# Sample's state updates moved up, the norms' roots split, sample's gates tied: one step of a hybrid decoder layer

## The chip, the cores and the metric

The kernel runs on one core of a Trainium2 chip. The metric is device time in microseconds: the median of several runs of the same program, and beside it one profiled execution, whose trace is the source of every row shown. Two programs are compared on the same chip.

## The reference

One inference step of a layer with two mixers. A prompt of 2048 tokens and a sample of 8 sequences of 8 new tokens go through the same weights.

```python
z = rmsnorm(x, norm_w) @ w_in
q, k, v, qb, kb, vb, g_lr, gate_a, gate_b = split(z)
o_a = attend(q, k, v)                      # three dilated windows, mixed by their softmax sums
log_a = log_sigmoid(g_lr @ w_gate_up + b_gate) / 16
o_b, s_fin = gla_chunked(qb / 8, kb, vb, log_a, s0)     # gated linear attention, 4 heads
o_b = rmsnorm(o_b, gla_norm_w)             # per head of 128
mixed = concat([o_a * silu(gate_a), o_b * silu(gate_b)])
y = x + mixed @ w_out
```

In the linear attention a state of 64 x 128 per head is decayed and added to: `state = exp(b_last) * state + k_decayed^T v`. For the prompt it starts at zero and runs over 16 chunks of 128 tokens; for the sample each of the 8 sequences brings its own state, reads it for its outputs, updates it once, and the new state is an output of the program. Each head's output then goes through a root mean square norm, so for every token and head a sum of squares and its inverse root are needed before the last projection.

## The kernel before

The program is one stream of operations written by Python generators. `weave` (L370) takes from several generators the one that is furthest behind its share, and so lays the parts into each other: a `host` (a projection on TensorE) with others beside it; a generator that yields WAIT is passed over. From this order a planner, which keeps its own clock of every engine, fixes the order of the instructions on each engine by when they can start. Each engine then runs its own instructions strictly in order; so does SP, which issues all DMAs.

Tiles live in pools. A pool takes a stretch of on-chip memory; a pool that is opened later can take the stretch of one that was closed. Tiles of one tag share a fixed number of buffers (`bufs`), and a new tile of a tag waits until the readers of the one that had its buffer are done.

The phases from 942 us on, which the change touches:

- **The gb projection** (942 to 1076 us). Host is `rest("gb")` (L1542): 16 prompt tiles through `project`, whose 24 matmuls per tile (L1161) add up `acc_gb`; ACT copies the result out (`zgb`, L757) and SP stores it. Beside it run the end of the prompt's linear attention (`gla_prompt`, with `chunk` for 128 tokens: state and output matmuls, the state's addition on DVE at L1331, and `gla_out`, which stores the output and takes the sums of squares of the four heads into columns of `ob_ss`, L346), the loading of the two halves of w_out (`load_w("o0")`, `load_w("o1")`, L664 and L665), and the sample's linear attention, `sample_gla` (L1400).
- **`sample_gla`** opens the pool sg1 and runs in this order: load the state S0, form decays and scores, then for each pair of heads p the outputs O_s (PSUM), their copy `ob_s` (L1467), store and sums of squares. Only when both pairs are done come the state updates (L1477 to L1503): for each pair p and half q of the sequences, and each head j, POOL builds a block `vx` of 64 x 4 x 128, in which each row holds its token's values in the place of its own sequence and zeros elsewhere (L1484); two matmuls (L1490) form U_s; POOL decays the old state (L1495) and DVE adds U_s (L1501). `vx` has one buffer. Two yields stand in each of the four rounds. After each pair SP stores the new state (L1506), and at the end sg1 is closed.
- **The seam** (L1553 to L1770). The five pools of the linear attention are closed, and cb (two buffers each) and cb1 (one) are opened in that stretch. cb1 holds, among others, `va`, `ob_rs`, `ident16`, the exponentials `sa`, and sample's own gates and outputs. `rsqrt` (L117) takes the 68 columns of `ob_ss` (4 for sample, 64 for 16 tiles) in one go to `ob_rs`: six small instructions, DVE, two on ACT (logarithm and exponential), three on DVE. `first_mixes` forms the mixes of tiles 0 and 1.
- **The output phase** (1102 us to the end). `prompt_out` (L1747) runs over the 16 tiles. `combine(t)` (L1680) loads the three attention branches (oc), gates (zl, `gates` L1579: a clamp on DVE, three passes on ACT into `sa`, two reductions on DVE, then `p2` and `smx`) and head outputs (obl, scaled by the roots on ACT, L1606), forms `mix`, and `parts_of` (L1612) splits it into two halves of 16 bits, mt: one ACT copy, one DVE subtraction. `turned` transposes mt on PE (tm, L1625) and ACT copies it out (mh, L1626); `finish` runs 48 matmuls Y (L1667) per tile, adds the residual on DVE (xr, L1674) and stores (L1678). Tile t+2 is combined while tile t is multiplied. At t = 8 in program order sample's gates and scaled outputs are formed (L1750); they are used before the last tile. Beside it runs sample's attention over its cache: keys (k, tk, L1842 and L1845), scores R, and values, 28 loads sv (L1922) into three buffers, each read by matmuls OS (L1896).

The planner brought sample's clamp and scaling forward, ahead of tile 0's matmuls: `zl_s` and `obl_s` in the trace.

Of the kernel before, what the change touches and what calls it, by code (L numbers as in the profile page):

```python
# [18 lines left out]
P = 128  # L19
# [33 lines left out]
def tile_hymba(ctx: ExitStack, tc: tile.TileContext, A: dict):  # L53
# [340 lines left out]
    with ExitStack() as c1:  # L394
# [867 lines left out]
        )  # L1262
        gpools = (gl, gt, ps_O, ps_S, ps_P, gq)

        masks = gc.tile([P, len(LEVELS), 32], F32, name="gmask")
        scan_m = gc.tile([P, 256], F32, name="scan_m")
        wgu = gc.tile([17, 256], F32, name="wgu")
# [28 lines left out]
        POOL.memset(ob_ss[:], 1.0)  # L1296

        def at_heads(t):
            c = 0 if t == "s" else 4 * (t + 1)
            return ob_ss[:, c : c + 4]  # L1300

        def chunk(core, gc):
            c, r0 = gc % 2, gc * P
            ebv = core.eb[:].rearrange("p a (c s) -> p a c s", s=P)
            vb = vbs.pop(gc)
            old, new = Sbd[gc % 2], Sbd[(gc + 1) % 2]
            U = ps_O.tile([P, 512], F32, name=f"U_{gc}", tag="O")
            for h in range(4):
                p, j = divmod(h, 2)
                PE.matmul(  # L1310
                    U[64 * j : 64 * j + 64, p * P : (p + 1) * P],
                    core.kdt[:, c, 64 * h : 64 * h + 64], vb[:, h * P : (h + 1) * P],
                    start=True, stop=True,
                )
            O = ps_O.tile([P, 512], F32, name=f"O_{gc}", tag="O")
            for p in range(2):
                if gc:
                    PE.matmul(
                        O[:, p * 256 : (p + 1) * 256], core.qe[:, p, c * P : (c + 1) * P],
                        old[:, p, :], start=True, stop=False,  # L1320
                    )
                for j in range(2):
                    h = 2 * p + j
                    PE.matmul(
                        O[:, h * P : (h + 1) * P], full[:, 4 * j + 2 * c + p, :],
                        vb[:, h * P : (h + 1) * P], start=(gc == 0), stop=(gc == 0 or j == 1),
                    )
            for p in range(2):
                for j in range(2):
                    sl = slice(64 * j, 64 * j + 64)  # L1330
                    DVE.scalar_tensor_tensor(  # L1331
                        new[sl, p, j * P : (j + 1) * P], old[sl, p, j * P : (j + 1) * P],
                        ebv[sl, p, c, P - 1 : P],
                        U[sl, p * P : (p + 1) * P], ALU.mult, ALU.add,
                    )
            gla_out(gq, O, P, r0, f"c{gc}", at_heads(gc))
            mixed.add(gc)

        vbs = {}

# [59 lines left out]
        def sample_gla():  # L1400
# [9 lines left out]
            yield from upto("vb", "s")  # L1410
            vb = g1.tile([NS, 512], F32, name="vb_s")
            SP.dma_start(vb[:], vb_d[S : S + NS, :])
            own = g1.tile([P, 512], F32, name="own", tag="vx")
            DVE.memset(own[:], 0.0)
            E, ks, qs = (
                own[:, 0:128].rearrange("p (i c) -> p i c", i=2), own[:, 128:256], own[:, 256:320]
# [26 lines left out]
            qe, eb, kdt, Am = core.qe, core.eb, core.kdt, core.Ac  # L1443
            so = A["state_gla_sample"][0]
            ebv = eb[:].rearrange("p a (b t) -> p a b t", t=8)
            for p in range(2):
                O = ps_O.tile([P, 512], F32, name=f"O_s{p}", tag="O")
                for j in range(2):
                    h, js = 2 * p + j, slice(64 * j, 64 * j + 64)
# [19 lines left out]
                for j in range(2):  # L1469
                    h = 2 * p + j  # L1470
                    jk = gq.tile([P, P], BF16, name=f"obq_s{h}", tag="obq", bufs=2)
                    ACT.activation(
                        jk[:NS], ob[:, j * P : (j + 1) * P], AF.Square,
                        accum_out=at_heads("s")[:NS, h : h + 1],
                    )
                yield
            for p in range(2):  # L1477
                for q in range(2):
                    sq = S0[p][:, 4 * q : 4 * q + 4, :]
                    U = ps_O.tile([P, 512], F32, name=f"U_s{p}{q}", tag="O")  # L1480
                    for j in range(2):
                        h = 2 * p + j
                        vx = g1.tile([NS, 4, P], F32, name=f"vx_{h}_{q}", tag="vx")
                        POOL.tensor_tensor(  # L1484
                            vx[:],
                            vb[:, h * P : (h + 1) * P].unsqueeze(1).to_broadcast([NS, 4, P]),
                            bm[:, 4 * q : 4 * q + 4].unsqueeze(2).to_broadcast([NS, 4, P]),
                            ALU.mult,
                        )
                        PE.matmul(  # L1490
                            U[64 * j : 64 * j + 64], kdt[:NS, 0, 64 * h : 64 * h + 64], vx[:],
                            start=True, stop=True,
                        )
                        if j == 0:
                            POOL.tensor_tensor(  # L1495
                                sq, sq,
                                ebv[:, p, 4 * q : 4 * q + 4, 7:8].to_broadcast([P, 4, P]),
                                ALU.mult,
                            )
                            yield  # L1500
                    DVE.tensor_tensor(  # L1501
                        sq, sq, U[:].rearrange("p (b v) -> p b v", b=4), ALU.add
                    )  # L1503
                    yield
                for j in range(2):
                    SP.dma_start(  # L1506
                        so[:, 2 * p + j].rearrange("b k v -> k b v"),
                        S0[p][64 * j : 64 * j + 64],
                    )
# [53 lines left out]
        va = cb1.tile([P, 2], F32, name="va")  # L1563
        for i, c_ in enumerate((2048.0 / M_SCALE, 1.0 / (P_SCALE * W_SCALE * H_SCALE * V_SCALE))):
            DVE.tensor_scalar(va[:, i : i + 1], powers["v"][:], c_, None, ALU.mult)
        ob_rs = cb1.tile([P, 4 * (NT + 1)], F32, name="ob_rs")
        rsqrt(cb1, ob_rs[:], ob_ss[:], 1.0 / 128.0, P, 4 * (NT + 1), "ob")

        def scales(c):

# [27 lines left out]
        def normed(t, n, rows):  # L1598

            pool, tag = (cb1, "obs") if t == "s" else (cb, "ob")  # L1600
            ob = pool.tile([P, 512], F32, name=f"obl_{t}", tag=tag)
            SP.dma_start(ob[:n], ob_d[rows, :])
            c = 0 if t == "s" else 4 * (t + 1)
            for h in range(4):
                s = slice(h * P, (h + 1) * P)
                ACT.activation(ob[:n, s], ob[:n, s], AF.Copy, scale=ob_rs[:n, c + h : c + h + 1])  # L1606
            return ob

        ident16 = cb1.tile([P, P], F16, name="ident16")
        DVE.tensor_copy(ident16[:], ident[:])  # L1610

        def parts_of(tag, mix):  # L1612

            mt = cb.tile([P, 2, D], F16, name=f"mt_{tag}", tag="mt")
            ACT.activation(mt[:, 0], mix[:], AF.Copy)
            DVE.tensor_tensor(mt[:, 1], mix[:], mt[:, 0], ALU.subtract)
            return mt

        def turned(tag, mt):
# [127 lines left out]
        def prompt_out():  # L1747
            for t in range(NT):
                rows = slice(t * P, (t + 1) * P)
                if t == NT // 2:  # L1750
                    at_s = slice(S, S + NS)
                    mixes["s"] = gates("s", NS, at_s), normed("s", NS, at_s)
                if t == NT - 1:
                    while "attended" not in mixed:
                        yield WAIT
# [289 lines left out]
```

## Time and profile before

| | |
|---|---|
| median of 3 runs | 1342.91 us (1339.44 to 1348.45) |
| the profiled execution, its own time | 1343.97 us |
| its span, first to last instruction | 1342.2 us |
| PE busy | 1210.9 us, 90% |
| DVE, ACT, POOL busy | 887.4, 848.5, 617.3 us |
| DMA | 285.39 MB, mean 213 GB/s |
| mean granted clock of TensorE | 0.977 |

Busy times are sums over the whole span; what a change is worth is read from the stage that it touches. In the rows below, `out<-in` are the program's names with numbers left out, L is a line of the kernel, `x16` a count; the bracket at the end is the idle time of that engine just before and what ended it. PEld is the loading of the stationary operand, SPq the queue of DMA issues. The shares of the DMA engines can come out a little over 1.

### The profile page before, as it was taken

Reading aid. Unit: us, or ns where it says so; the run is one execution under the profiler, and the core shown is the slowest. Engines: PE = TensorE matmul, PEld = TensorE weight load, DVE = VectorE, ACT = ScalarE, POOL = GpSimd, SP = SyncE. Lnnn points to the kernel's source line nnn. Section 1 sums busy time; section 2 is a strip of 40 time slices with the busy share of each in tenths; the row PEclk is TensorE's granted clock in tenths of the full one; section 3 lists DMA queues with packets and bytes.
Section 4 is the critical chain, followed back from the end, with each engine's and each line's share of the span. In section 5 each row is a group of like instructions: output and inputs, shape, how many; then the busy total and the mean of one; then the engine's idle time right before and its main releaser. Section 6 shows DMA issues by size and latency. Waiting matters only on the chain.

```text
span 1342.2 us, 27996 instructions
## 1 busy us (share of the span) xinstructions
PE 1210.9 (90%) x9754; PEld 727.2 (54%) x9754; DVE 887.4 (66%) x2317; ACT 848.5 (63%) x2281; POOL 617.3 (46%) x596
## 2 busy tenths in 40 slices
PE   3798999999899798998999988899999949999998
PEld 1343565566556545666677665567555424544443
DVE  6357767788868937678672885666542368889741
ACT  5655787878669858787895454455762366556520
POOL 0066554687758733654222865665423123233210
PEclk9999999999999999999999999999999969999999
DMA  8959866668955798989785564553552688898752
GB/s 259 253 155 243 227 190 150 179 208 225 223 173 177 210 271 285 264 265 227 199 200 174 185 217 124 165 147 108 149 200 84 233 273 294 303 384 319 298 187 79
DMA packets 251807, 285.39 MB, mean 213 GB/s; under 512 B 125441, under 2 KB 160338, under 8 KB 251666
## 3 DMA queue, kind: packets, MB, share of 16 engines
q1 hardware_dynamic: 251666, 283.60, 70.6%
q8 instruction: 77, 1.26, 0.4%
q14 instruction: 64, 0.52, 0.1%
HBM read 183.12 MB, written 75.24 MB: 192 GB/s over the span
## 4 chain that ended last, share of the span: by engine, by line
PE 44%; DVE 13%; DMA 10%; POOL 8%; issue 7%; ACT 5%; SPq 1%; POOLq 0%; DVEq 0%; ACTq 0%
PE acc_gb L1161 6%; PE Y L1667 6%; PE acc_qkb L1161 4%; PE acc_vb L1161 3%; PE acc_g L1161 3%; DMA T<-qp_d 3%; PE O L492 3%; PE s L459 2%; PE t L477 2%; PE acc_k L1161 2%; POOL k L1027 2%; PE acc_q L1161 2%; PE acc_v L1161 2%; PE sc_e L289 2%; DVE p L467 1%
## 5 line engine op out<-in xcount | busy, mean ns | idle before, releaser
L1161 PEld LDWEIGHTS <-hr 128*128 128x128 f16 x1824 | 174.5, 99 | 128.8 <-issue 13.2
L1161 PEld LDWEIGHTS <-hl 128*128 128x128 f16 x1248 | 121.5, 99 | 148.5 <-issue 24.4
L444 POOL TENSOR_TENSOR pt<-p,pt 128x512 f16<-128x512 f32 (+1 forms) x80 | 94.0, 1175 | 224.3 <-ACT pt L443 187.0
L470 ACT ACTIVATE p<-p,o 128x256 f32<-128x256 f32 (+1 forms) x320 | 148.5, 468 | 52.2 <-DVE o L467 50.7
L1667 PE MATMUL Y<-w_o,mh 128*128 128x512 f16 x768 | 176.4, 379 | 2.7 <-DVE xr L1674 1.6
L1027 POOL TENSOR_TENSOR k<-k,qb 128x512 f32<-128x512 f32 x96 | 132.2, 1391 | 27.9 <-DMA qb<-q_d 12.3
L1667 PEld LDWEIGHTS <-mh 128*128 128x128 f16 x768 | 71.6, 98 | 89.6 <-issue 9.9
L477 PE MATMUL t<-ident,p 128*128 128x128 f32 x600 | 107.6, 281 | 6.6 <-ACT p L470 2.9
L492 PEld LDWEIGHTS <-pt 128*128 128x128 f16 x1200 | 82.7, 99 | 47.1 <-issue 9.5
L492 PE MATMUL O<-v,pt 128*128 128x128 f16 x944 | 88.6, 223 | 20.6 <-POOL pt L444 6.1
L467 DVE CUSTOM_DVE_ANT_0 p<-s,m3w,scl_s 128x128 f32<-128x128 f32 (+1 forms) x256 | 89.2, 395 | 26.0 <-PE s L459 7.4
L1161 PE MATMUL acc_g<-w_g,hr 128*128 128x272 f16 (+1 forms) x768 | 103.4, 282 | 3.1 <-ACT vbs L761 3.1
L1161 PE MATMUL acc_v<-w_v,hl 128*128 128x512 f16 x384 | 95.0, 391 | 9.1 <-DMA hl<-early_ht 4.5
L1709 POOL TENSOR_TENSOR tc<-oc,w 128x512 f32<-128x512 f32 x32 | 44.9, 1422 | 113.7 <-DVE w L1701 87.3
L1161 PE MATMUL acc_k<-w_k,hl 128*128 128x512 f16 x384 | 93.1, 379 | 4.2 <-ACT zs_k L692 2.9
L238 POOL TENSOR_TENSOR D_e<-b_e 128x512 f32<-128x512 f32 x56 | 62.4, 1118 | 72.1 <-ACT E L244 54.8
L1161 PE MATMUL acc_q<-w_q,hl 128*128 128x512 f16 x384 | 92.1, 387 | 3.2 <-ACT zs_k L692 1.9
L1161 PE MATMUL acc_vb<-w_vb,hr 128*128 128x512 f16 x384 | 92.4, 382 | 0.0
L1161 PE MATMUL acc_gb<-w_gb,hr 128*128 128x512 f16 x384 | 87.9, 380 | 0.0
L244 ACT ACTIVATE E<-D_e 128x256 f32<-128x256 f32 x112 | 43.7, 417 | 64.1 <-DVE ks L249 42.8
L459 PE MATMUL s<-kk,qq 128*128 128x256 f16 (+1 forms) x512 | 78.4, 266 | 5.2 <-DVE o L467 3.1
L477 PEld LDWEIGHTS t<-ident,p 128*128 128x128 f32 x600 | 69.7, 144 | 20.6 <-ACT p L470 11.2
(513 smaller groups left out, 2651.0 us busy)
## 6 DMA issues: line engine op xcount, KB each, us to landing
k<-in_cache_k_win SPq DMA_DIRECT2D x104, 256.0 KB
sv<-in_cache_v_win SPq DMA_DIRECT2D x24, 1024.0 KB
hr<-h_d SPq DMA_DIRECT2D x44, 512.0 KB
qb<-q_d SPq DMA_DIRECT2D x64, 256.0 KB
oc<-o_d SPq DMA_DIRECT2D x48, 264.0 KB
o_d<-o SPq DMA_DIRECT2D x80, 132.0 KB
x<-in_x_prompt SPq DMA_DIRECT2D x16, 512.0 KB
h_d<-hl SPq DMA_DIRECT2D x16, 512.0 KB
```

Of the source, the lines that this page charges most:

```text
L238: dec = POOL.tensor_tensor(dv, bv, bv[:, :, 0:1, B - 1 : B].to_broadcast([P, M, 2, B]), ALU.subtract)
L244: ACT.activation(ev[:, half], dv[:, :, half, :], AF.Exp, scale=(2 * half - 1) / 16.0)
L444: pins["POOL"] = POOL.tensor_tensor(l, f, h, ALU.subtract).ins
L459: PE.matmul(s_ps[:, i * w : (i + 1) * w], q, k, start=(n == 0), stop=(n == len(prods) - 1),)
L467: DVE.tensor_tensor_reduce(s[:, sl], s_ps[:, sl], mask, neg, BIG, ALU.add, ALU.min, nmf(i))
L470: ACT.activation(s[:, sl], s[:, sl], AF.Exp, bias=nmf(i), scale=-1.0, accum_out=denf(i))
L477: PE.transpose(p_ps[:, i * P : (i + 1) * P], t["s"][:, i * P : (i + 1) * P], ident[:])
L492: PE.matmul(o_, t["pt"][:, c, (i * nb + b) * P : (i * nb + b + 1) * P], vf(i, b), start=(n == 0), stop=(n == 2 * nb - 1),)
L1027: POOL.tensor_tensor(pr[:], k_[:], sk_state["q", t][:], ALU.mult)
L1161: PE.matmul(z, a_[:, k, :], w[:, p_, k, cols], start=(k == 0 and i == 0), stop=(k == KT - 1 and i == 2),)
L1667: PE.matmul(Y[:], a_[:, k, :], w_[:, part, k, :512], start=(i == 0), stop=(i == len(prods) - 1),)
L1709: eng.tensor_tensor(t_[:], oc[:, g, :, 0:64], w[:, g].unsqueeze(2).to_broadcast([P, NH, HD]), ALU.mult,)
```

## The change

Three edits.

1. In `sample_gla` the state updates of a pair of heads follow straight behind the outputs of that pair. The four blocks vx of the pair are built ahead of its outputs, `vx` has four buffers (the first tile of the tag, `own`, is one of them), the two matmul pairs of a round stand together, and both decays of the pair follow the outputs. One yield per round is left.
2. The columns of `ob_ss` are put in another order (tiles first, sample last), and the roots are taken in place in two batches: columns 0 to 31, which are tiles 0 to 7, in `chunk` when chunk 9 is through, with scratch tiles in the pool gc; columns 32 to 67 at the seam, with scratch tiles in cb1. `ob_rs` is gone.
3. `parts_of` keeps its two instructions in `marks`, and sample's gates and scaled outputs are traced under `issue_after` for those of tile 2, the third tile: on ACT and on DVE they are queued behind them.

```diff
         def at_heads(t):
-            c = 0 if t == "s" else 4 * (t + 1)
+            c = 4 * (NT if t == "s" else t)
             return ob_ss[:, c : c + 4]
+
+        def head_scales(pool, c):
+            rsqrt(pool, ob_ss[:, c], ob_ss[:, c], 1.0 / 128.0, P, c.stop - c.start, f"ob{c.start}")
...
             gla_out(gq, O, P, r0, f"c{gc}", at_heads(gc))
             mixed.add(gc)
+            if gc == 9:
+                head_scales(gc_pool, slice(0, 32))
...
-            own = g1.tile([P, 512], F32, name="own", tag="vx")
+            own = g1.tile([P, 512], F32, name="own", tag="vx", bufs=4)
...
+            def block(p, q, j):
+                h = 2 * p + j
+                vx = blocks[p, q, j] = g1.tile([NS, 4, P], F32, name=f"vx_{h}_{q}", tag="vx", bufs=4)
+                POOL.tensor_tensor(
...
             for p in range(2):
+                for q in range(2):
+                    for j in range(2):
+                        block(p, q, j)
                 O = ps_O.tile([P, 512], F32, name=f"O_s{p}", tag="O")
...
+                for q in range(2):
+                    sq = S0[p][:, 4 * q : 4 * q + 4, :]
+                    POOL.tensor_tensor(
+                        sq, sq, ebv[:, p, 4 * q : 4 * q + 4, 7:8].to_broadcast([P, 4, P]), ALU.mult
+                    )
                 yield
-            for p in range(2):
                 for q in range(2):
                     sq = S0[p][:, 4 * q : 4 * q + 4, :]
                     U = ps_O.tile([P, 512], F32, name=f"U_s{p}{q}", tag="O")
                     for j in range(2):
                         h = 2 * p + j
-                        vx = g1.tile([NS, 4, P], F32, name=f"vx_{h}_{q}", tag="vx")
-                        POOL.tensor_tensor(
...
-                        )
+                        PE.matmul(
+                            U[64 * j : 64 * j + 64], kdt[:NS, 0, 64 * h : 64 * h + 64],
+                            blocks.pop((p, q, j))[:], start=True, stop=True,
+                        )
...
-        ob_rs = cb1.tile([P, 4 * (NT + 1)], F32, name="ob_rs")
-        rsqrt(cb1, ob_rs[:], ob_ss[:], 1.0 / 128.0, P, 4 * (NT + 1), "ob")
+        head_scales(cb1, slice(32, 4 * (NT + 1)))
...
+            rs = at_heads(t)
             for h in range(4):
                 s = slice(h * P, (h + 1) * P)
-                ACT.activation(ob[:n, s], ob[:n, s], AF.Copy, scale=ob_rs[:n, c + h : c + h + 1])
+                ACT.activation(ob[:n, s], ob[:n, s], AF.Copy, scale=rs[:n, h : h + 1])
...
+            marks[tag] = (
+                ACT.activation(mt[:, 0], mix[:], AF.Copy).ins,
+                DVE.tensor_tensor(mt[:, 1], mix[:], mt[:, 0], ALU.subtract).ins,
+            )
...
                 if t == NT // 2:
                     at_s = slice(S, S + NS)
-                    mixes["s"] = gates("s", NS, at_s), normed("s", NS, at_s)
+                    with ExitStack() as order:
+                        for m_ in marks[2]:
+                            order.enter_context(tc.issue_after(m_))
+                        mixes["s"] = gates("s", NS, at_s), normed("s", NS, at_s)
```

More of the change, by code (lines that the diff above doesn't have):

```diff
@@ L1263, in tile_hymba @@
         gpools = (gl, gt, ps_O, ps_S, ps_P, gq)
+        gc_pool = gc
         masks = gc.tile([P, len(LEVELS), 32], F32, name="gmask")
@@ L1445, in sample_gla @@
             ebv = eb[:].rearrange("p a (b t) -> p a b t", t=8)
+            blocks = {}
+            def block(p, q, j):
+                h = 2 * p + j
+                vx = blocks[p, q, j] = g1.tile([NS, 4, P], F32, name=f"vx_{h}_{q}", tag="vx", bufs=4)
+                POOL.tensor_tensor(
+                    vx[:],
+                    vb[:, h * P : (h + 1) * P].unsqueeze(1).to_broadcast([NS, 4, P]),
+                    bm[:, 4 * q : 4 * q + 4].unsqueeze(2).to_broadcast([NS, 4, P]),
+                    ALU.mult,
+                )
             for p in range(2):
+                for q in range(2):
+                    for j in range(2):
+                        block(p, q, j)
                 O = ps_O.tile([P, 512], F32, name=f"O_s{p}", tag="O")
@@ L1482, in sample_gla @@
                         h = 2 * p + j
-                        vx = g1.tile([NS, 4, P], F32, name=f"vx_{h}_{q}", tag="vx")
[L1484 to L1488, printed above, removed]
-                        )
-                        PE.matmul(
-                            U[64 * j : 64 * j + 64], kdt[:NS, 0, 64 * h : 64 * h + 64], vx[:],
-                            start=True, stop=True,
-                        )
[L1494 to L1500, printed above, removed]
+                        PE.matmul(
+                            U[64 * j : 64 * j + 64], kdt[:NS, 0, 64 * h : 64 * h + 64],
+                            blocks.pop((p, q, j))[:], start=True, stop=True,
+                        )
                     DVE.tensor_tensor(
@@ L1602, in normed @@
             SP.dma_start(ob[:n], ob_d[rows, :])
-            c = 0 if t == "s" else 4 * (t + 1)
+            rs = at_heads(t)
             for h in range(4):
                 s = slice(h * P, (h + 1) * P)
-                ACT.activation(ob[:n, s], ob[:n, s], AF.Copy, scale=ob_rs[:n, c + h : c + h + 1])
+                ACT.activation(ob[:n, s], ob[:n, s], AF.Copy, scale=rs[:n, h : h + 1])
             return ob
@@ L1610, in tile_hymba @@
         DVE.tensor_copy(ident16[:], ident[:])
+        marks = {}
         def parts_of(tag, mix):
             mt = cb.tile([P, 2, D], F16, name=f"mt_{tag}", tag="mt")
-            ACT.activation(mt[:, 0], mix[:], AF.Copy)
-            DVE.tensor_tensor(mt[:, 1], mix[:], mt[:, 0], ALU.subtract)
+            marks[tag] = (
+                ACT.activation(mt[:, 0], mix[:], AF.Copy).ins,
+                DVE.tensor_tensor(mt[:, 1], mix[:], mt[:, 0], ALU.subtract).ins,
+            )
             return mt
```

## The prediction

> **What bounds the kernel now.** I read the table of windows first, cut at the phases of the program. Columns: length, then busy time of PE, PEld, DVE, ACT and POOL, the granted clock, the DMA share, GB/s.
>
> ```profile
> 942.00:1076.40 134.40, 134.40 (x1143) 72.13 (x1142) 53.35 (x150) 67.52 (x196) 40.13 (x47) 1.00 0.51 165
> 1076.40:1102.50 26.10, 8.35 (x72) 5.65 (x72) 16.18 (x44) 15.82 (x31) 8.64 (x8) 0.61 0.93 280
> 1102.50:1150.00 47.50, 47.50 (x345) 22.24 (x346) 40.72 (x104) 29.51 (x48) 16.74 (x13) 1.00 0.89 325
> 1150.00:1200.00 50.00, 48.01 (x364) 23.52 (x363) 40.47 (x105) 30.16 (x49) 13.94 (x11) 1.00 0.88 324
> 1200.00:1250.00 50.00, 49.52 (x389) 24.66 (x388) 41.92 (x111) 30.93 (x50) 16.84 (x12) 1.00 0.92 344
> 1250.00:1300.00 50.00, 47.42 (x351) 22.34 (x350) 36.74 (x86) 20.62 (x30) 12.90 (x9) 1.00 0.66 248
> ```
>
> PE is the bound on both sides of one hole. In the gb projection (942 to 1076.4), beside which sample's GLA runs, it is busy for all of 134.4 us; in the output phase it misses 0, 2.0, 0.5 and 2.6 us of four windows. Between them, from 1076.4 to 1102.5, it works 8.35 of 26.1 us: 17.75 us idle. Work moved about inside 942 to 1076.4 is worth nothing by itself; what counts is what starts behind it.
>
> Next the timeline of the hole and the stretch ahead of it (start, duration, engine, line, operation, count, idle time before and its releaser).
>
> ```profile
> 1030.72 0.38 ACT L1467 ACTIVATE ob_s<-O_s 64x256 f32<-64x256 f32 x1 [11.13 <-PE O_s L1462]
> 1055.24 1.39 SPq L1684 DMA_DIRECT2D oc<-o_d  x3
> 1063.55 0.68 DVE L1585 TENSOR_SCALAR zl<-zl 128x1024 f32<-128x1024 f32 x1
> 1073.31 1.07 PE L1490 MATMUL U_s<-vx,kdt_smp 64*64 64x512 f32 x2
> 1074.41 0.69 DVE L1501 TENSOR_TENSOR S<-S,U_s 128x512 f32<-128x512 f32 x1 [6.23 <-PE U_s L1490]
> 1075.02 0.21 DVE L1565 TENSOR_SCALAR va<-pw_v 128x1 f32<-128x1 f32 x2
> 1075.14 0.19 DVE L122 TENSOR_SCALAR rv_ob<-ob_ss 128x68 f32<-128x68 f32 x1
> 1075.24 0.22 DVE L1610 CAST ident<-ident 128x128 f16<-128x128 f32 x1
> 1076.51 0.69 ACT L757 ACTIVATE zgb<-acc_gb,wi_gb 128x512 f32<-128x512 f32 x1 [5.60 <-PE acc_gb L1161]
> 1077.10 1.05 ACT L1587 ACTIVATE sa<-zl 128x1024 f32<-128x1024 f32 x1
> 1078.04 0.25 ACT L123 ACTIVATE rr_ob<-rv_ob 128x68 f32<-128x68 f32 x1
> 1085.09 0.61 DVE L1808 COPY qx<-ts_q 64x128 f32<-64x128 f32 x2 [3.32 <-PE ts_q L1796]
> 1088.15 2.55 POOL L1709 TENSOR_TENSOR tc<-oc,w 128x512 f32<-128x512 f32 x2 [5.20 <-DVE w L1701]
> 1094.28 1.06 ACT L1615 ACTIVATE mt<-mix 128x1024 f16<-128x1024 f32 x1 [4.63 <-DVE mix L1716]
> 1095.79 1.09 PE L1845 MATMUL tk<-ident,k 128*128 128x128 f32 x4 [8.65 <-DMA k<-in_cache_k_win]
> 1099.06 1.28 ACT L1606 ACTIVATE obl_s<-obl_s,ob_rs 64x128 f32<-64x128 f32 x4 [0.27 <-DMA obl_s<-ob_d]
> 1102.47 6.43 PE L1667 MATMUL Y<-w_o,mh 128*128 128x512 f16 x29 [1.09 <-ACT mh L1626]
> ```
>
> The first output tile is late. Its loads are issued from 1055.24 and its gates clamped at 1063.55, but the exponentials of the same gates (sa) run at 1077.10, though ACT idled 5.60 us just before. What separates the two is the pool: zl and oc lie in cb, sa in cb1. Everything that writes a cb1 tile (va, rv_ob, ident16, sa) first appears after the last state addition of sample (S, 1074.41). I take this as the gate: cb1 opens only when sample's state tiles are given back. Adding up the tile sizes, the five GLA pools hold 76,448 bytes per partition and cb with cb1 76,480, so cb1 reaches 32 bytes into the place where sg1, sample's pool, stands. From sa to the steady run of Y is 1102.47 - 1077.10 = 25.4 us.
>
> The waits of PE in that stretch name something else:
>
> ```profile
> PE tk L1845 <- DMA k<-in_cache_k_win: 8.7, 1, 8.7
> PE R L1822 <- POOL Scg L1817: 6.6, 1, 6.6
> ```
>
> Those are sample's attention steps standing in PE's queue while there was no Y to run. I read them as fillers of the hole, not its cause; that they are the cause is the first rival.
>
> **Why the state is late.**
>
> ```profile
> L1490 PE MATMUL U_s<-vx,kdt_smp x16: 589/589/640, 1023.4 to 1073.8; 64*64 64x512 f32 x16
> L1484 POOL TENSOR_TENSOR vx<-vb_s,bm x8: 1032/1032/1034, 1005.5 to 1068.2; 64x512 f32<-64x512 f32 x8
>   PE U_s L1490: 31.8, 6
> ```
>
> Eight blocks vx share one buffer, so each POOL product waits for the matmul pair that read the block before: 31.8 us in 6 waits, the pairs strewn from 1023.4 to 1073.8.
>
> **The change, part by part.**
>
> *State updates behind each pair of heads, four buffers.* Counts stay: 8 POOL blocks of 1.03 us, 16 U_s matmuls, 4 decays, 4 additions, 2 pairs of stores. The round trip goes, and so do four of the eight yields between the pairs. Sample's second outputs left PSUM at 1030.72 before (ob_s), so I expect the last addition by 1050 at the latest and not 1074.4. On PE and POOL the moved work is free: PE is full until 1076.4 either way, and POOL is busy for 40.1 of 134.4 us. What is queued behind the blocks on POOL is GLA's own differences and queries; three blocks (3 x 1.03) and three pairs of matmuls (3 x 1.07) now run ahead of GLA's last chunk, which could end by up to 6 us later and push the loads of 1055.24 with it. Bounds 0 to 6; I take 0, since POOL is 70% idle there.
>
> *The stores of the state* leave SP's queue where they stood at 1075, ahead of sample's first loads; earlier they ride beside a DMA share of 0.51. No term.
>
> *Roots in two batches.* Six instructions of 0.19 to 0.25 us over 68 columns become twice six over 32 and 36: at most 6 x 0.25 = 1.5 us more on DVE and ACT together, in phase 942 to 1076.4, under a full PE: nothing. It also takes ob_rs and half of three scratch tiles out of cb1 (672 bytes with padding) and adds 384 to gc, so cb and cb1 (75,808) now end inside the GLA pools (76,832). So two edits open cb1 independently: sg1 is given back sooner, and cb1 no longer reaches it. Either way it should open with cb, at 1055.
>
> *Sample's gates behind tile 3.* The clamp (on DVE) and the four obl_s scalings (1.28 us on ACT, standing ahead of tile 0's mh) move behind the third tile's mt. Their three loads on SP are not tied and stay. Worth 1.3 us in the chain of tile 0.
>
> **The sum.** The chain of tile 0 now starts behind its clamp, 1063.55 + 0.68 = 1064.2. Of its 25.4 us two pieces fall away: DVE's wait behind qx (3.32, which stood between the gates' reduction and p2; that work will be done before ts_q exists) and obl_s (1.28). 25.4 - 4.6 = 20.8, so Y runs at 1085.0. PE has then 8.6 us behind the gb phase, and work for part of it:
>
> ```profile
> L1625 PE MATMUL tm<-ident,mt 128*128 128x128 f16 x16 | 1.9, 295 | 0.0
> L1822 PE MATMUL R<-ident,Scg 128*128 128x128 f32 x2 | 0.7, 444 | 6.6 <-POOL Scg L1817 6.6
> L1796 PE MATMUL ts_q<-ident,ls_q 64*128 64x64 f32 x4 | 0.7, 325 | 0.6 <-DMA ls_q<-q_d 0.6
> L1796 PE MATMUL ts_k<-ident,ls_k 64*128 64x64 f32 x4 | 0.7, 324 | 0.3 <-DMA ls_k<-k_d 0.3
> L1830 PE MATMUL R<-ksT,qx 128*32 128x64 f32 x16 | 0.7, 315 | 0.5 <-ACT ksT L1802 0.5
> L1845 PE MATMUL tk<-ident,k 128*128 128x128 f32 x8 | 2.1, 424 | 8.7 <-DMA k<-in_cache_k_win 8.7
> L1625 PE MATMUL tm<-ident,mt 128*128 128x128 f16 x240 | 18.1, 219 | 0.0
> L1845 PE MATMUL tk<-ident,k 128*128 128x128 f32 x24 | 4.0, 275 | 0.0
> ```
>
> (The first six rows are of the hole, the last two of the phase behind it.) tm and the four sample groups make 4.7 us, so 3.9 us stay idle: 17.75 - 3.9 = 13.9 won. Bounds: 0 idle if the chain is over by 1076.4, and 12.2 idle under the first rival.
>
> Second term: the hole's small matmuls ran slowly, at a granted clock of 0.61. A key transpose took 2.1/8 = 0.26 us there against 4.0/24 = 0.17 later, a tm 0.119 against 0.075: 0.8 and 0.7 us for these two groups. I take 1.5, bounds 0 and 3 (twice that, if the groups without a later twin slowed alike). [...]
>
> Third: what the output phase does with an earlier start. Its PE work is unchanged. DMA has slack between the bursts of cache loads:
>
> ```profile
> 1129.00:1142.00 13.00, 13.00 (x112) 5.62 (x103) 10.04 (x26) 8.06 (x9) 4.13 (x4) 1.00 1.03 390
> 1155.00:1168.00 13.00, 13.00 (x89) 6.75 (x88) 8.89 (x30) 10.70 (x18) 2.47 (x2) 1.00 0.66 237
> ```
>
> Bursts at 390 GB/s with PE full, pauses at 237. I take 0, bounds -2 (some of the later idle goes too) and +6 (one load that lands late, 5.95 in the row of the third rival).
>
> Sum: 13.9 + 1.5 = 15.4. The profiled execution took 1343.97 us for a span of 1342.2; the median of the runs, 1342.91, is 1.06 below it. So the new span is 1326.8, its execution 1328.6, the median **1327.5 us**. The likeliest case's own range is 1320 to 1335: 7.5 less with no idle hole, a full clock and 2 us of later idle gone, as much more with GLA 6 us late.
>
> **Rivals.** A measurement of this kernel can tell about 1% from no change.
>
> *Sample's keys keep PE's queue (0.13).* PE works in order. If the key transposes still stand ahead of tile 0's Y, Y waits for the keys, whose load landed only at 1095.79 and hangs on hp (in use to 1076.4) and on SP. For it: the 8.7 us above. Against: those keys entered PE's queue when no tile was ready, and an order laid out by readiness will put Y first. Y from 1095.79 + 1.09 = 1096.9 instead of 1102.5: 5.6 us, 1337.3.
>
> *The hole stays: cb1 opens late for another reason (0.08).* For it: sa directly follows zgb, the last projected tile's copy, so the gate could be ACT's order. Against: va and rv_ob on DVE have nothing to do with zgb and are as late. 1342.9.
>
> *Slower: stores block the cache loads (0.06).* SP issues in order, and a y store waits there for its tile:
>
> ```profile
> SPq L1678 <- DVE xr L1674: 35.5, 8, 10.5
> ```
>
> ```profile
> 1285.22 5.95 DMA sv<-in_cache_v_win
> ```
>
> The second row (of the chain that ended last) is such a load, issued right behind a store. With Y some 15 us ahead of the cache loads, one such stall of 5.95 in each of the four pairs of sequences costs 23.8 against 15.4 won: 1351.3. It decides from the third on (17.9). Against: DMA's pauses, and loads that run three buffers ahead.
>
> **How the numbers follow.** The hole closes 0.73, and the three rivals 0.13, 0.08, 0.06. Range 1320 to 1341: the forecast's own and the first rival; outside are the second, the third and a thin tail below. Under 1329.5 (1% faster) lies about four fifths of the likeliest case: 0.58. Over 1356.3 only a worse third rival: 0.04. The rest, 0.38, is within 1%.
>
> **What would show it.** Right: the last S addition before 1055; sa of tile 0 near 1064, ahead of the last zgb; the steady Y from 1080 to 1087; PE idle in the hole 1 to 6 us; the same PE total less 1 to 3. Wrong: sa again behind the last zgb (second rival), or a PE wait of 5 us or more for the keys ahead of Y (first), or more than 6 us of PE waits for sv (third).

## The result, and the profile after

| | before | after |
|---|---|---|
| median | 1342.73 us (1339.44 to 1348.45, 4 runs) | 1329.04 us (1325.76 to 1334.30, 4 runs) |
| the profiled execution, its own time | 1343.97 us | 1326.84 us |
| its span | 1342.2 us | 1325.0 us |

The ratio is 0.9897, 95% interval 0.9848 to 0.9947: 13.8 us faster, 7 to 20. The forecast of 1327.5 us is 1.5 away. A second comparison (below) gave 0.9886, 0.9864 to 0.9908. The ratios are worked out by themselves and not from the two medians shown, so they can differ a little from their quotient.

The two spans differ by 17.2 us, more than the medians. To see where, the span is cut at the gb projection. Its first and last matmul, in the view of the tile acc_gb (count, durations in ns, first and last start): before, then after.

```profile
L1161 PE MATMUL acc_gb<-w_gb,hr x384: 379/379/390, 945.0 to 1076.0; 128*128 128x512 f16 x192
```

```profile
L1161 PE MATMUL acc_gb<-w_gb,hr x384: 379/379/391, 937.5 to 1064.0; 128*128 128x512 f16 x192
```

Three pieces: 7.5 us arise ahead of the phase (945.0 to 937.5), 4.5 inside it (131.0 long before, 126.5 after), and 5.2 behind it (266.2 to the end of the span before, 261.0 after).

**Inside the phase.** The state updates, by tile, in after. The last addition of the state is at 1030.5 where before had 1074.4, and the blocks vx wait 1.3 us in 2 waits for the matmuls, not 31.8 in 6:

```profile
L1508 PE MATMUL U_s<-vx,kdt_smp x16: 589/589/640, 1002.4 to 1029.8; 64*64 64x512 f32 x16
L1512 DVE TENSOR_TENSOR S<-S,U_s x4: 680/689/689, 1008.8 to 1030.5; 128x512 f32<-128x512 f32 x4
```

```profile
  PE U_s L1508: 1.3, 2
```

Sixteen records of 589 ns, as before. But the time in which PE was at work on them, from the table of windows cut down to the tile U_s (length, then PE, PEld, DVE), is 8.50 us before and 4.74 after:

```profile
940.00:1075.00 135.00, 8.50 (x16) 1.56 (x16) 2.65 (x4) 1.00 0.52 166
```

```profile
940.00:1075.00 135.00, 4.74 (x16) 1.24 (x16) 2.75 (x4) 0.97 0.58 179
```

The timeline shows how. Before, one block's two records stand alone and take 1.07 us; after, the four of a round are through in 1.13 us (1029.40 + 1.02 - 1029.29):

```profile
1073.31 1.07 PE L1490 MATMUL U_s<-vx,kdt_smp 64*64 64x512 f32 x2
```

```profile
1029.29 0.64 PE L1508 MATMUL U_s<-vx,kdt_smp 64*64 64x512 f32 x1
...
1029.40 1.02 PE L1508 MATMUL U_s<-vx,kdt_smp 64*64 64x512 f32 x3
```

**The seam.** Timeline of after, from the clamp of tile 0's gates to the steady Y:

```profile
1051.89 0.69 DVE L1595 TENSOR_SCALAR zl<-zl 128x1024 f32<-128x1024 f32 x1
...
1055.65 1.05 ACT L1597 ACTIVATE sa<-zl 128x1024 f32<-128x1024 f32 x1
...
1065.20 0.67 ACT L757 ACTIVATE zgb<-acc_gb,wi_gb 128x512 f32<-128x512 f32 x1
...
1067.71 0.49 SPq L1810 DMA_DIRECT2D ls_q<-q_d  x1
...
1071.65 1.06 ACT L1628 ACTIVATE mt<-mix 128x1024 f16<-128x1024 f32 x1 [4.18 <-DVE mix L1730]
...
1074.60 0.69 PE L1813 MATMUL ts_q<-ident,ls_q 64*128 64x64 f32 x4 [10.21 <-DMA ls_q<-q_d]
...
1075.32 1.23 DVE L1825 COPY qx<-ts_q 64x128 f32<-64x128 f32 x4 [0.46 <-PE ts_q L1813]
...
1076.45 1.04 PE L1639 MATMUL tm<-ident,mt 128*128 128x128 f16 x8
...
1076.58 1.23 DVE L1629 TENSOR_TENSOR mt<-mix,mt 128x1024 f16<-128x1024 f32 x1
...
1079.68 1.91 PE L1681 MATMUL Y<-w_o,mh 128*128 128x512 f16 x4
...
1082.05 2.32 PE L1681 MATMUL Y<-w_o,mh 128*128 128x512 f16 x10
```

sa now runs 9.5 us ahead of the last zgb. But PE stands for 10.21 us, the whole rest of the hole: at the head of its queue is the transpose of sample's new queries, whose load ls_q was issued only at 1067.71. Tile 0's first half (mt on ACT) is ready at 1072.7 and waits on PE behind it; its second half waits on DVE behind the copies qx. So ls_q alone holds PE only for the last 1.9 us of the wait (1072.7 to 1074.60). In the 8.3 us before that, tile 0 was not ready either.

Behind the phase, windows of 30 and 200 us (columns as in the prediction), before and after:

```profile
1076.40:1106.40 30.00, 12.25 (x90) 7.43 (x90) 19.32 (x53) 19.72 (x40) 8.64 (x8) 0.66 0.94 293
1106.40:1306.40 200.00, 194.96 (x1463) 94.13 (x1462) 157.46 (x394) 109.27 (x168) 60.42 (x44) 1.00 0.81 301
1306.40:1342.20 35.80, 30.30 (x155) 13.90 (x153) 7.41 (x11) 2.60 (x4) 0.00 (x0) 1.00 0.21 74
```

```profile
1064.40:1094.40 30.00, 19.80 (x136) 11.51 (x137) 20.85 (x53) 14.14 (x23) 14.15 (x14) 0.77 0.96 302
1094.40:1294.40 200.00, 192.06 (x1444) 92.76 (x1443) 147.76 (x382) 105.56 (x169) 51.67 (x41) 0.99 0.82 298
1294.40:1325.00 30.60, 25.16 (x126) 11.39 (x124) 6.66 (x10) 2.60 (x4) 0.00 (x0) 0.99 0.21 69
```

PE's idle time falls from 17.75 to 10.20 us in the first 30, and rises from 5.04 to 7.94 in the next 200. Its work, summed over the three, is 237.51 and 237.02. From the phase's start to the end the profile thus has 4.5 + 7.55 - 2.90 + 0.49 = 9.6 of the 9.7 us.

### The profile page after: what moved, and what is told of

It reads as the page before. It is cut to its first block, busy times and chain, and to the rows that moved or that the text cites. A ratio compares the mean times of both kernels' runs of the same rounds, so it can differ in the third digit from the quotient of the medians.

```text
span 1325.0 us, 27988 instructions
## 1 busy us (share of the span) xinstructions
PE 1199.1 (90%) x9754; PEld 722.9 (55%) x9754; DVE 885.7 (67%) x2321; ACT 847.7 (64%) x2283; POOL 612.7 (46%) x596
## 5 line engine op out<-in xcount | busy, mean ns | idle before, releaser
L1723 POOL TENSOR_TENSOR tc<-oc,w 128x512 f32<-128x512 f32 x32 | 41.0, 1300 | 169.8 <-DVE w L1715 169.8
```

Of the source, the lines that this page charges most:

```text
L1723: eng.tensor_tensor(t_[:], oc[:, g, :, 0:64], w[:, g].unsqueeze(2).to_broadcast([P, NH, HD]), ALU.mult,)
```

## The experiments

Each kernel from state only on was timed beside runs of before of its own. The table reads them all in the same way: start, length and end of gb from the row of acc_gb; "behind" is the span less the last start of acc_gb; Y is the first Y less the same (the expectations speak of the steady Y, which can come later); idle is the window less PE's busy time in it, for the 30 us and the next 200 behind the phase. The columns from "gb starts" on are of one profiled execution each, which need not lie near the median: that of state only took 1333.12 us, the longest of its six, and that of after again 1322.55, the shortest of its six.

| kernel | median us | ratio to before, 95% | gb starts | gb long | behind | Y | idle 30 | idle 200 |
|---|---|---|---|---|---|---|---|---|
| before | | | 945.0 | 131.0 | 266.2 | 23.8 | 17.75 | 5.0 |
| after | 1329.04 | 0.9897 (0.9848 to 0.9947) | 937.5 | 126.5 | 261.0 | 15.7 | 10.2 | 7.9 |
| state only | 1327.20 | 0.9901 (0.9875 to 0.9926) | 941.3 | 126.5 | 263.5 | 14.9 | 11.4 | 8.7 |
| roots in place | 1338.69 | 0.9997 (0.9981 to 1.0013) | 942.1 | 131.0 | 264.6 | 17.3 | 10.9 | 9.1 |
| spare tile | 1339.13 | 1.0009 (0.9985 to 1.0033) | 935.2 | 131.0 | 267.7 | 25.1 | 19.1 | 5.3 |
| queries behind | 1325.51 | 0.9911 (0.9884 to 0.9939) | 935.4 | 126.5 | 262.0 | 14.0 | 9.8 | 7.6 |
| after again | 1325.74 | 0.9886 (0.9864 to 0.9908) | 931.5 | 126.5 | 262.8 | 15.8 | 10.3 | 10.0 |
| same half | 1329.56 | 0.9912 (0.9890 to 0.9933) | 943.8 | 129.9 | 256.6 | 15.8 | 10.3 | 4.7 |
| new early | 1328.62 | 0.9900 (0.9875 to 0.9925) | 941.0 | 127.3 | 259.8 | 10.3 | 8.1 | 9.1 |
| GLA denser | 1322.89 | 0.9863 (0.9842 to 0.9885) | 937.4 | 127.3 | 257.0 | 11.0 | 7.5 | 7.5 |
| buffers only | 1328.90 | 0.9918 (0.9895 to 0.9941) | 938.7 | 127.2 | 257.9 | 7.5 | 5.9 | 8.7 |
| gates untied | 1327.96 | 0.9919 (0.9891 to 0.9946) | 936.7 | 126.6 | 259.1 | 14.9 | 9.1 | 6.8 |

My theory when they began: cb1 was shut by 32 bytes that lay in sg1's place, either of two edits opens it, and the hole that is left is PE's wait for ls_q. Rivals: the late state itself makes tile 0 late; or what the hole wins is given back.

### State only

The first edit alone: `ob_rs`, its one batch of roots and the untied gates are as before.

> The kernel before with the first edit alone: state updates behind each pair of heads, four block buffers; roots in one batch (cb1 as large as before), sample's gates not tied. My theory (cb1 was shut by sg1, and early updates close sg1): sa of tile 0 by 1060, ahead of the last zgb; from the last gb tile's matmul to the steady Y 17 to 20 us where before shows 26.1; U_s busy 4.7 us of PE where before shows 8.5, so that the gb phase is 3.8 us shorter; median 1329 to 1333. Rival (the roots in two batches, by making cb1 smaller, are what opens it): sa stays behind the last zgb, the hole stays 26 us, only the 3.8 us of the gb phase are won, 1339.

Measured: sa 8.3 us ahead of the end of gb (1059.5 against 1067.8), gb 126.5, the steady Y 17.5 us behind the phase (1085.74 against 1068.2), 0.9901; the median, 1327.20, is 2 us under the range given. The first theory: the first edit brings the measurable gain.

### Roots in place, and the spare tile

Before, with the tile `ob_rs` taken away:

```diff
-        ob_rs = cb1.tile([P, 4 * (NT + 1)], F32, name="ob_rs")
-        rsqrt(cb1, ob_rs[:], ob_ss[:], 1.0 / 128.0, P, 4 * (NT + 1), "ob")
+        rsqrt(cb1, ob_ss[:], ob_ss[:], 1.0 / 128.0, P, 4 * (NT + 1), "ob")
...
-                ACT.activation(ob[:n, s], ob[:n, s], AF.Copy, scale=ob_rs[:n, c + h : c + h + 1])
+                ACT.activation(ob[:n, s], ob[:n, s], AF.Copy, scale=ob_ss[:n, c + h : c + h + 1])
```

> The kernel before with one line less: the roots are written into ob_ss itself, so that the tile ob_rs (272 bytes of a partition) leaves cb1. No other edit; the state stays late. My theory (32 bytes of cb1 lay where sg1 stands): cb1 opens with cb, sa of tile 0 runs ahead of the last zgb and near 1060 although the last state addition stays near 1074; the gb phase keeps its 130.4 us; the hole falls from 26.1 us to some 18 and the median to 1334 to 1338. Rival (the late state updates themselves, in the queues of PE, POOL and DVE, make tile 0 late): sa stays near 1077, 1341 to 1344.

The other run gives cb1 its length back:

```diff
+        spare = cb1.tile([P, 4 * (NT + 1)], F32, name="spare")
+        DVE.memset(spare[:, 0:1], 0.0)
         rsqrt(cb1, ob_ss[:], ob_ss[:], 1.0 / 128.0, P, 4 * (NT + 1), "ob")
```

> As the run with the roots in place, with a spare tile of 272 bytes in cb1 where ob_rs stood (one column of it is set, nothing reads it). My theory: cb1 is again 32 bytes too long, sa of tile 0 again behind the last state addition, near 1077, the hole again 26 us, 1341 to 1344. Rival (writing in place saves something by itself): as the run without the spare tile, 1334 to 1338.

The timeline of the run in place. The first cb1 tile of the roots is written at 1053.31, 18 us ahead of the last state addition, and sa of tile 0 runs at 1063.14:

```profile
1053.31 0.20 DVE L122 TENSOR_SCALAR rv_ob<-ob_ss 128x68 f32<-128x68 f32 x1 [0.57 <-ACT obq_c L346]
...
1063.14 1.04 ACT L1586 ACTIVATE sa<-zl 128x1024 f32<-128x1024 f32 x1
...
1071.44 0.69 DVE L1501 TENSOR_TENSOR S<-S,U_s 128x512 f32<-128x512 f32 x1 [2.24 <-PE U_s L1490]
...
1083.21 0.69 PE L1795 MATMUL ts_q<-ident,ls_q 64*128 64x64 f32 x4 [9.76 <-DMA ls_q<-q_d]
```

With the spare tile both stand behind that addition again:

```profile
1064.56 0.69 DVE L1501 TENSOR_TENSOR S<-S,U_s 128x512 f32<-128x512 f32 x1 [6.03 <-PE U_s L1490]
...
1065.30 0.19 DVE L122 TENSOR_SCALAR rv_ob<-ob_ss 128x68 f32<-128x68 f32 x1
...
1067.24 1.05 ACT L1588 ACTIVATE sa<-zl 128x1024 f32<-128x1024 f32 x1
```

So the gate is shown: 272 bytes of a tile that nothing reads decide whether tile 0's gates wait for the state. Its worth came out smaller than I had forecast. Without the spare tile 8.2 us of idle time go from the first 30 us, 3.8 come back in the next 200, PE's work grows by 1.1 (237.44 to 238.52), and the stretch behind gb is 3.1 shorter; the ratios, 0.9997 against 1.0009, are 1.6 us apart with intervals that hold both this and nothing. I had expected 5 to 9.

Roots in place and state only both open cb1 early, yet their ratios are 0.9997 and 0.9901. So by the medians most of the gain comes with the early state updates and not with the gate. The two profiles show 5.6 us of it: 4.5 in the gb phase and 1.1 behind it (264.6 against 263.5). The rest they do not show.

### Queries behind

After, with the new queries and keys behind the last steps of tile 0 that exist when they are emitted:

```diff
+            with ExitStack() as order:
+                for m_ in marks[0]:
+                    order.enter_context(tc.issue_after(m_))
+                sample_new()
```

Here `marks[0]` also holds the last transpose tm.

> The kernel after, with sample's queries and keys of its new tokens (ls_q, ls_k, their transposes and copies) issued behind tile 0's mt on ACT and DVE and behind its last tm on PE. My theory (what is left of the hole is PE's wait of 10.2 us for ls_q, which stands ahead of tile 0's tm, and DVE's qx copies ahead of its mt): steady Y some 12 to 14 us behind the gb phase where after shows 17.6; 1323 to 1326. Rival (tile 0's own chain from sa to mt ends as late without them): Y stays 16 to 18 us behind, 1328 to 1330.

Measured: the first Y, with which the steady run begins here, starts 13.6 us behind the phase (1075.90 against 1062.3), and the median is 1325.51, 0.9911: both lie where my theory had them. But the idle time is 9.8 us, against 10.2 in after. The waits of PE behind the phase:

```profile
PE R L1840 <- POOL Scg L1835: 6.3, 1, 6.3
...
PE tm L1639 <- ACT mt L1628: 1.7, 1, 1.7
PE tm L1639 <- DVE mt L1629: 1.6, 1, 1.6
```

The wait for ls_q is gone and three others have its place: the next of sample's steps in PE's queue (R, for masks), and tile 0's own halves. Of the 10.2 us only 0.4 were won. The steady Y came sooner because sample's scores R for the new keys and its key transposes tk, which in after stand ahead of it, now stand behind it, and not because PE waited less. So the numbers were the theory's, but the idle time that it put down to ls_q stayed. Tile 0's first half is ready 8.7 us behind the phase (1069.89 + 1.06), no sooner than the 8.3 in after, as the rival had it.

### After again, and the same half

After again is the control for the runs that follow.

> The kernel after once more, timed beside the three others of this call. Both theories: gb phase (first to last acc_gb) 126.5 us as in after's profile, stretch from there to the end 261 us, median 1326 to 1332. The start of the gb phase, which lay at 935 to 945 us in kernels whose program is the same up to there, may lie anywhere in that range.

The phase took 126.5 us, as expected; the stretch was 262.8, 1.8 longer, and the median, 1325.74, lies just under the range. The other kernel lays both heads into the same 64 rows of U, and so leaves out half of sample's state update:

```diff
-                            U[64 * j : 64 * j + 64], kdt[:NS, 0, 64 * h : 64 * h + 64],
+                            U[0:64], kdt[:NS, 0, 64 * h : 64 * h + 64],
...
-                        sq, sq, U[:].rearrange("p (b v) -> p b v", b=4), ALU.add
+                        sq[:64], sq[:64], U[:64].rearrange("p (b v) -> p b v", b=4), ALU.add
```

> The kernel after, with the state update of the second head of a pair written over that of the first, into the same 64 of PE's columns, and the addition over these 64 rows alone: it leaves out half of sample's state update. Same number of matmuls and additions. Theory A (the gb phase became 4.5 us shorter because the two heads' U_s matmuls, now adjacent, run side by side in the two halves of PE's columns): the four matmuls of a group take some 2.2 us instead of 1.1, the gb phase is back at 130 to 131 us, the median some 4 us above after's. Theory B (the saving comes from fewer changes between kinds of matmul, or from the order of the rest): gb phase stays 126.5, median as after's.

The four adjacent matmuls of a round now take 1.88 us instead of 1.13, and the tile U_s 7.54:

```profile
1037.58 1.88 PE L1508 MATMUL U_s<-vx,kdt_smp 64*64 64x512 f32 x4
```

```profile
940.00:1075.00 135.00, 7.54 (x16) 1.94 (x16) 2.72 (x4) 1.00 0.54 172
```

The phase is 129.9 us long, 3.4 of the 4.5 back: in after, where each head writes its own half of U, four records of 589 ns were through in 1.13 us, and in one half they took 1.88. That the halves of PE's columns make the difference was my theory and is not shown by itself: laid into one half, the matmuls also write to the same place in PSUM, and this run does not tell the two apart. What the other 1.1 us are was not tried. The medians, 1329.56 against 1325.74, lie as theory A has it, but the intervals overlap and the profiled executions from gb's start to the end are 386.5 and 389.3; the phase, not the total, carries this finding: behind it the planner laid the output phase's matmuls in another order than after's, so the two ends do not compare.

### New early, and GLA denser

After, with sample's loads in cb1 where they need not wait for the last pools, the first pair's transposes behind tile 0's mt and tm, and three fills behind tile 0's sum on POOL:

```diff
+            ls[nm_] = cb1.tile([NS, 512], F32, name=f"ls_{nm_}")
+            SP.dma_start(ls[nm_][:], src[S : S + NS, :])
...
-                x = ssk.tile([NS, 512], F32, name=f"ls_{nm_}", tag="k1")
-                SP.dma_start(x[:], src[S : S + NS, :])
+                x = ls[nm_]
...
+            with behind(bp):
...
+        with tc.issue_after(summed[0]):
+            POOL.memset(P3x[:], 0.0)
```

> The kernel after, with sample's new queries and keys (ls_q, ls_k) loaded into cb1 before the gb phase ends, and with the first pair's transposes of masks and keys, and POOL's three fills, behind tile 0's own steps. Theory A (what is left of the hole is worth its length): no PE wait above 3 us ahead of Y but for tile 0's own chain, steady Y 11 to 13 us behind the gb phase instead of 17.6, stretch behind the gb phase 255 to 257 us, median 4 to 5 us under after's. Theory B (the output phase gives back what the hole wins, as with the roots in place, where Y came 9 us sooner and the end 2 us): Y sooner, stretch still 259 to 262 us, with more PE waits later for sv, mh or k1T; median within 2 us of after's.

The first Y came 10.3 us behind gb and the steady Y 13.8 behind the phase (1082.49 against 1068.7), where after has 17.6 and theory A 11 to 13. Ahead of Y PE waited for nothing but tile 0's chain:

```profile
PE tm L1643 <- ACT mt L1632: 7.8, 1, 7.8
```

So the theory with which the runs began fails here: with ls_q out of the way PE still waits 7.8 us, for tile 0's first half. The idle time in the first 30 us is 8.1, in the next 200 it is 9.1, and the stretch behind gb, 259.8, lies in theory B's range; the median, 1328.62, is 2.9 us above that of after again. That is nearer to theory B: nothing was won that these runs can tell. The second kernel adds

```diff
-        late.append([sample_gla(), 32])
-        gla_all = [gla_all[0], 32]
+        late.append([sample_gla(), 42])
+        gla_all = [gla_all[0], 42]
```

> As the run with the new queries early, and the steps of GLA and of sample's GLA woven in more densely (42 per round where 32 stood), so that GLA's pools are given back sooner and tile 0's chain starts sooner. Theory A: zl of tile 0 loaded some 10 us sooner against the end of the gb phase, steady Y 3 to 8 us behind the gb phase, stretch 250 to 255 us, median 7 to 10 us under after's. Theory B (given back): Y sooner, stretch 258 to 262, median within 2 us of after's.

Its load zl was issued no sooner (18.7 us ahead of gb's end, 18.0 in the run without the denser steps) and Y no sooner, so theory A's mechanism did not happen. Still it had the lowest median of the study, 1322.89, and 0.9863 (0.9842 to 0.9885): faster than before, and 2.9 us under after again, with intervals that overlap. Why it is better than the run before it stays open; by the profile it idles 1.6 us less in the 200 us behind the first 30.

### Buffers only

Before, with two numbers:

```diff
-            own = g1.tile([P, 512], F32, name="own", tag="vx")
+            own = g1.tile([P, 512], F32, name="own", tag="vx", bufs=4)
...
-                        vx = g1.tile([NS, 4, P], F32, name=f"vx_{h}_{q}", tag="vx")
+                        vx = g1.tile([NS, 4, P], F32, name=f"vx_{h}_{q}", tag="vx", bufs=4)
```

> The kernel before with four vx buffers instead of one and nothing else: the loops, the roots in one batch and sample's gates stay. Theory A (the round trip through one block buffer made the state late; the place of the loop matters less): last state addition by 15 us or more ahead of the end of the gb phase instead of 1.6, the two heads of a group adjacent on PE and so the gb phase at 126.5 to 128 us, sa of tile 0 ahead of the last zgb, median within 3 us of after's, 1325 to 1331. Theory B (the yields between the pairs keep the state late and the pool shut): last addition within 5 us of the gb phase's end, hole as before, at most the 4.5 us of the gb phase won, 1336 to 1342.

The state is through 18.5 us ahead of gb's end (1047.4 against 1065.9), and U_s is adjacent, 4.49 us of PE:

```profile
L1501 DVE TENSOR_TENSOR S<-S,U_s x4: 686/689/690, 1018.3 to 1047.4; 128x512 f32<-128x512 f32 x4
```

In the planned order tile 0's tm and Y now stand ahead of sample's transposes, so the load that holds PE in after holds it nowhere:

```profile
1071.03 1.03 PE L1625 MATMUL tm<-ident,mt 128*128 128x128 f16 x8 [4.80 <-DVE gmax_b L1591]
...
1073.40 6.11 PE L1667 MATMUL Y<-w_o,mh 128*128 128x512 f16 x23
...
1079.58 0.46 PE L1796 MATMUL ts_q<-ident,ls_q 64*128 64x64 f32 x4
```

```profile
1066.30:1096.30 30.00, 24.12 (x148) 12.67 (x149) 22.33 (x53) 15.54 (x24) 13.39 (x13) 0.89 0.92 299
1096.30:1296.30 200.00, 191.35 (x1447) 93.87 (x1445) 147.14 (x379) 103.66 (x165) 53.66 (x41) 0.99 0.84 300
1296.30:1323.80 27.50, 22.28 (x113) 10.09 (x111) 5.91 (x9) 2.65 (x4) 0.00 (x0) 1.00 0.21 67
```

The hole is down to 5.9 us, the smallest of all. The median, 1328.90, is 3.2 above that of after again, which was timed beside other runs of before; the ratios' intervals, 0.9895 to 0.9941 and 0.9864 to 0.9908, overlap. Theory A: the buffers carry the change, and the move of the loop adds nothing that these runs can tell.

### Gates untied

> The kernel after without its third edit: sample's gates and scalings are not tied behind tile 3's mt. Theory A (obl_s and the clamp of sample's gates stood in the chain of tile 0, 1.3 us): first 30 us behind the gb phase with 11 to 12 us of idle PE instead of 10.2, median 0 to 3 us above after's. Theory B (PE's wait for ls_q covers them): 10 to 10.5 us idle, median within 1 us of after's.

After without the third edit: idle 9.1 us, neither theory's number and not more than after's. The median is 1 us below after's first measurement and 2 above its second. The third edit's 1.3 us do not show.

## Why the prediction was right, and where it was not

The time was right, and so was the reason why cb1 opens. The sum was not, and that its total is only 1.5 us off is luck in good part. Of its 15.4 us the profile shows 9.7 from gb's start on: the hole gave 6.3 less than forecast, the output phase took back 2.9 and the clock gave 1.0 less, against 4.5 that the sum had put at nothing. What the median has beyond these 9.7 us is not located.

- **The gate** (32 bytes of cb1 in sg1's place; two edits that each open it). Right: the pair roots in place and spare tile shows that the length of cb1 decides, and state only that early updates open it too. The 32 bytes themselves are a sum of tile sizes; the runs show that taking 272 away is enough. What it brings alone is small: 1.6 us by the ratios, not told from nothing.
- **The state late through one buffer.** Right: the last addition by 1050 was forecast, it came at 1030.5, and two numbers alone bring it to 18.5 us ahead of gb's end.
- **"Work moved about inside 942 to 1076.4 is worth nothing by itself."** This step failed: 4.5 us. The change altered what stands next to what. One block buffer had kept the two heads' matmuls apart, 8.50 us of PE; with four they are adjacent and overlap, 4.74 us. The traces show 1.13 us for four records that write two halves of U (after) and 1.88 in one half (same half); the prediction had quoted the row of two such matmuls, 1.07 us, and had not asked what two heads side by side would take.
- **3.9 us of idle time left in the hole, 13.9 won.** This step failed too: 10.2 left, 7.55 won (10.35 left in the second profile of after). The working took tile 0's chain for the limit and sample's small steps for fillers. Where the chain starts came out: the clamp ended 11.8 us ahead of the phase's end (1052.58 against 1064.4), and 12.2 had been taken. Its length did not: 20.8 us were taken from the clamp to the steady Y, and after took 29.5, or 27.1 to the first Y. Where sample's steps stand behind tile 0 it takes 20.6 (buffers only, 1052.85 to 1073.40), so the length was right for tile 0 alone. In after the planner put sample's steps first, the transposes of ls_q above all, whose load was issued only 3.3 us behind the phase (1064.4 to 1067.71). That is the first rival's mechanism, a step of sample ahead of Y in PE's order, with another load than the one named there (ls_q, not the cache keys). But it is not the whole hole: even a Y 20.6 us behind the clamp would have come 8.8 us behind the phase, and new early, without that step, still idles 8.1.
- **Taking the wait away is not all gain.** Queries behind and new early do so and win 0.4 and 2.1 us of the first 30; their ratios, 0.9911 and 0.9900, are no lower than after's 0.9897 and 0.9886.
- **The later output phase, 0, bounds -2 to +6.** +2.90 and, in after again, +4.95 (190.01 us busy of 200). Inside the bounds, and seen in most profiles: nine of the ten in which cb1 opens early idle 6.8 to 10.0 us there, the two in which it opens late 5.0 and 5.3. The tenth, same half, idles 4.7: the planner laid its Y and OS matmuls in another order than after's. And after and after again, with the same order on every engine, differ by 2.1 us. So the price depends on the planned order as well, and a single profile gives it to some 2 us. The third rival's loads are not the cause, 0.6 us of waits for sv where before has 2.6; the waits in after are spread over mh, k1T and spr, of which before shows none behind its first 30 us. The first view is of before, the second of after, with the wait in the hole at its head:

```profile
PE OS L1896 <- DMA sv<-in_cache_v_win: 2.6, 3, 1.8
```

```profile
PE ts_q L1813 <- DMA ls_q<-q_d: 10.2, 1, 10.2
PE Y L1681 <- ACT mh L1640: 2.9, 3, 2.2
PE R L1847 <- DVE k1T L357: 2.5, 2, 1.4
PE T L1892 <- ACT spr L1879: 1.8, 1, 1.8
...
PE OS L1913 <- DMA sv<-in_cache_v_win: 0.6, 1, 0.6
```

- **The clock, 1.5.** PE's work behind gb fell by 0.49 us (237.51 to 237.02), and the granted clock of the first 30 us rose from 0.66 to 0.77. A shorter hole did not bring more: in buffers only the granted clock of the first 30 us is 0.89 where before had 0.66, and the work sums to 237.75 us, no less than before's 237.51.
- **Roots at nothing, gates at 1.3 us.** Neither can be told from zero here. The first batch of roots runs ahead of the gb phase, not in it as I wrote:

```profile
893.42 1.12 DVE L122 TENSOR_SCALAR rv_ob<-ob_ss 128x32 f32<-128x32 f32 x1 [0.49 <-ACT obq_c L346]
```

- **The signs.** The early last addition and the early sa came as given. Idle time of 1 to 6 us in the hole did not, 10.2, nor did a PE total less by 1 to 3; it is 11.8 less (1210.9 before), 6.8 of it ahead of gb, where the two programs have PE do the same, and 4.5 in the gb phase:

```profile
PE 1199.1 (90%) x9754; PEld 722.9 (55%) x9754; DVE 885.7 (67%) x2321; ACT 847.7 (64%) x2283; POOL 612.7 (46%) x596
```

  Steady Y, given for 1080 to 1087, came at 1082.05, but for the wrong reason: the hole was longer than forecast and gb ended 12 us sooner. A time counted from the start of the span mixes both; the distance from gb's end, 17.6 us, does not.

What stays open. From the start of gb to the end the profile of after is 9.7 us shorter than before's; the medians say 13.8 (7 to 20) and 15.3 (12 to 18). The 7.5 us of the profile that lie ahead of gb need not come from the change: the spare tile's order of instructions is before's on PE, POOL and SP, and its gb starts at 935.2, 9.8 us sooner:

```profile
L1161 PE MATMUL acc_gb<-w_gb,hr x384: 378/379/391, 935.2 to 1066.2; 128*128 128x512 f16 x192
```

The start is at 945.0, 942.1 and 935.2 with the late state and at 931.5 to 943.8 in the nine profiles with the early one. On average it comes a little sooner in these nine (938.1 against 940.8), and from there to the end they take 10.1 less (387.1 against 397.2); their spans are 12.7 us shorter, near the medians' difference. So most of the gain lies from gb's start on, and one pair of profiles is too few to divide it further. Whether the few us ahead of gb are of the change could not be told. Nor is it settled why an earlier Y makes the later phase idle more; that sample's steps of the first pair once stood in the hole for nothing, and now stand between the Y matmuls, is argued and not shown.

## What to carry to other kernels

Ask of a moved matmul not only what hides it but what will stand beside it: here small matmuls that write different halves of a tile cost little more than half as much when nothing stood between them (4.74 us against 8.50). When a hole closes, read the queue of the waiting engine in the new order, since here the next instruction whose input was late took the wait over (10.2 us for ls_q in after, 6.3 for the masks' R in queries behind, 7.8 for tile 0's mt in new early); and ask when the work behind it would have been ready, since only the time from there on is that instruction's (1.9 of the 10.2 us in after). And measure from the nearest common event, not from the start of the program, when two profiles are compared.

## What the hardware showed that I had not expected

- Four matmul records of 64*64 by 64x512 took 1.13 us in the last round of after (1.06 to 1.27 over its four) when they wrote two halves of U's rows, 1.88 in one half (same half), and two alone took 1.07 (before); the median record shows 589 ns in before and in after.
- The same order of instructions reached the gb phase at 945.0 us in one execution and at 935.2 in another (before and spare tile), while the phase itself was 131.0 us long in both.
